# Input tiles at one place modulo 256 bytes, and entries with plain fp32 products, in a two-layer decoder trunk

## The chip, the cores and the metric

The kernel runs on one core of one Trainium2 chip. The metric is the time of one execution on the device in microseconds (us); the smaller the better. Each kernel is run several times and the median is given.

## What is computed

The reference is a causal decoder trunk of two layers on 256 tokens of width 2048, in fp32. Each layer is a mixer and an MLP with a squared relu, each behind an RMS norm with a shift, a scale and a gate from a conditioning vector:

```python
def sqrelu_mlp(h, w1, w2):
    return jnp.square(jax.nn.relu(h @ w1)) @ w2

cond = jax.nn.silu(c)
for l in range(DEPTH):                      # 2
    mod = cond @ ada_w[l] + ada_b[l]        # 2048 -> 6 * 2048
    sh1, sc1, g1, sh2, sc2, g2 = [m[:, None, :] for m in jnp.split(mod, 6, axis=-1)]
    h = rms_norm(x, norm1_g[l]) * (1.0 + sc1) + sh1
    if l % 2 == 0:                          # mLSTM and retention heads
        y = mlstm_retention_mixer(h, even_w_in[e], ..., even_w_out[e])
    else:                                   # sparse attention, 16 query heads
        y = dsa_mixer(h, odd_w_in[o], ..., rel_bias, odd_w_out[o])
    x = x + g1 * y
    h = rms_norm(x, norm2_g[l]) * (1.0 + sc2) + sh2
    x = x + g2 * sqrelu_mlp(h, mlp_w1[l], mlp_w2[l])     # 2048 -> 8192 -> 2048
return x
```

Nearly all of the work is in the linear maps: the input and output projections of the two mixers, the two MLPs, and the conditioning's `ada_w`.

## The kernel before

**Split products.** The kernel computes in a transposed layout: a tile has 128 features on the partitions and the T = 256 tokens in the free dimension. fp32 values are split into a high part in fp32r (a type of four bytes, whose matmuls leave one record each in the trace, where plain fp32 leaves two) and the remainder, also in fp32r. An input tile `hs` (`hs_tile`, L201) holds the high part of 128 features in columns 0 to 255 and the low part in columns 256 to 511. A weight load (`wload`, L235) brings a `raw` tile of 128 x 1024 by DMA on SP's queue; `wsplit` (L226) makes `wh` of it on ScalarE (L230) and `wl` on VectorE (L232). A product is then hi x hi + hi x lo + lo x hi, made by matmuls that all pass through `mm` (L124), in three forms:

- `tmul` (L247), in the MLPs: `wh` stays in the array (the stationary tile), and the 512 columns of `hs`, high and low, stream past it; then `wl` against the 256 high columns. Two matmuls, of 512 and of 256 columns.
- `nmul2` (L281), in the other linear maps and for the last column tiles of the MLP's w2: three matmuls of 256 columns (`wh` x high, `wh` x low, `wl` x high).
- `nmul` (L308), in the last product (`result`, L597: the second MLP's w2, so that the output stands by token) and in the value projections (`linear_n`): a piece of `hs` of 128 columns is stationary, and 512 columns of `wh` or `wl` stream past it. Three matmuls of 512 columns.

`linear` (L252) walks over the contraction index k, one or two k for each weight load, and lets a batch of two loads wait for each other at the end (`stag`).

**Stages.** Layer 0's projections and heads, its output projection (`residual`, `out_groups`), MLP 0 (`mlp`: w1 in 16 groups of 512 columns, then w2 in two groups of eight column tiles), layer 1's projections and attention, its output projection, MLP 1 (w1, then `result`). Between them stand three *entries* (`entry`, L499): the first group of MLP 0's w1, of layer 1's input projection and of MLP 1's w1. At an entry the RMS norm is not known yet, so the first 8 k are multiplied without it: `Norm.plain` makes tiles u = x times a scale column, with the two parts of the shift beside them as two more columns, and `umul` (L494) does three matmuls of 258, 256 and 258 columns. The result is scaled by the norm afterwards, and the shift's sums are added (L532, L533, L537). `Norm.lengths` computes the norm with two tiny matmuls of `ssq` and one of `diag` (L196). The other 8 k come as usual.

**Where tiles lie.** Pools hand out fixed slots in SBUF. `hsp` has 16 slots for `hs` tiles, used in turn; a tile is 2T + 2 floats long (the two columns of the shift), which makes a slot of 2080 bytes, so that the 16 slots start at 224, 0, 32, 64, 96, 128, 160 and 192 modulo 256 bytes, each on two of them, and successive tiles go down by 32. The tags `raw`, `wh` and `wl` have four slots each, all of which start at 224 modulo 256. These places are read from the program as built.

**Order.** Each engine runs its instructions in the order in which the scheduler put them at build time; a tile's slot is written again only when its last reader is done. `Fill` (a generator of conditioning work: DMAs `ada`, and VectorE folds `acc`, L395) is called once for each weight load and spreads a given number of folds over a given number of calls, its `slots`.

Of the kernel before, what the change touches and what calls it, by code (L numbers as in the profile page):

```python
# [18 lines left out]
P = 128  # L19
# [75 lines left out]
def tile_trunk(ctx: ExitStack, tc: tile.TileContext, io, out):  # L95
# [105 lines left out]
    def hs_tile():  # L201
        return hsp.tile([P, 2 * T + 2], F32R, tag="hs", name="hs")

    def split_to_hs(src):
        h = hs_tile()
        S.copy(h[:, 0:T], src)  # L206
        V.tensor_tensor(h[:, T:2 * T], src, h[:, 0:T].bitcast(F32), op=OP.subtract)  # L207
        return h
# [16 lines left out]

    def wsplit(raw, n):  # L226
        wh = wp.tile([P, 1024], F32R, tag="wh", name="wh")
        wl = wp.tile([P, 1024], F32R, tag="wl", name="wl")
        with tc.high_priority(offset=60):
            S.copy(wh[:, :n], raw[:, :n])  # L230
            with held_back():
                last_split[0] = V.tensor_tensor(wl[:, :n], raw[:, :n], wh[:, :n].bitcast(F32), op=OP.subtract)  # L232
        return wh, wl

    def wload(W, k0, kper, cols):  # L235

        w = sum(c1 - c0_ for c0_, c1 in cols)
        raw = wp.tile([P, 1024], F32, tag="raw", bufs=4, name="raw")
# [6 lines left out]
        return wsplit(raw, kper * w)  # L245
# [189 lines left out]
    class Norm:  # L435
# [17 lines left out]
        def plain(self, l, n):  # L453


            sh = shift(l, 3 * n)
            s2 = small.tile([P, 8, 2], F32R, tag="sh2", bufs=1, name="sh2")
            S.copy(s2[:, :, 0], sh[:, 0:8])
            V.tensor_tensor(s2[:, :, 1], sh[:, 0:8], s2[:, :, 0].bitcast(F32), op=OP.subtract)
            us = []  # L460
            for k in range(8):
                u, a = hs_tile(), acol[:, l, n, k:k + 1]
                S.activation(u[:, 0:T], xT[:, k, :], AF.Copy, scale=a)
                S.copy(u[:, T:T + 2], s2[:, k, :].bitcast(F32))
                V.scalar_tensor_tensor(u[:, T + 2:], xT[:, k, :], a, u[:, 0:T].bitcast(F32), op0=OP.mult, op1=OP.subtract)
                us.append(u)
# [27 lines left out]
    def umul(o, u, wh, wl, c, m, start, stop):  # L494
        mm(o[0:m, 0:T + 2], wh[:, c:c + m], u[:, 0:T + 2], start=start, stop=False)
        mm(o[0:m, 0:T], wh[:, c:c + m], u[:, T + 2:2 * T + 2], start=False, stop=False)
        mm(o[0:m, 0:T + 2], wl[:, c:c + m], u[:, 0:T + 2], start=False, stop=stop)

    def entry(W, cols, tiles, norm, l, n, held, late, out, done, fill):  # L499
# [4 lines left out]
        ws = {}  # L504

        def load(k0):
            ws[k0] = wload(W, k0, 2, cols)
            fill()

        for k0 in (0, 2, 4):  # L510
            load(k0)
        norm.lengths(last_split[0].ins)
        hs, sums_ = [None] * KT, []
        for k0 in range(0, KT, 2):
            if k0 not in ws:
                load(k0)
            wh, wl = ws[k0]
            for q, (c, m) in enumerate(tiles):
                for kk in range(2):
                    k = k0 + kk  # L520
                    if k < 8:
                        umul(held[q], us[k], wh, wl, kk * w + c, m, k == 0, k == 7)
# [3 lines left out]
            if k0 == 6:  # L526
                for k in range(8, KT):
                    hs[k] = norm.normed(l, n, k)
                for q, (c, m) in enumerate(tiles):
# [3 lines left out]
                    V.tensor_tensor(s[0:m], b[0:m, T + 1:T + 2], s[0:m], op=OP.add)  # L533
# [91 lines left out]
    def mlp(l, before, fill, norm):  # L625
        with ExitStack() as es:
# [13 lines left out]
            def squared(i, a):  # L640
# [3 lines left out]
            free[:] = [3]  # L644
            hs = entry(io["mlp_w1"][l], [(0, 512)], [(j * P, P) for j in range(4)], before, l, 1,
                       [bank(0), bank(1), bank(2), lbank()], [lbank(), lbank()], [ztile(i) for i in range(4)],
                       lambda q: squared(q, z[q]), fill)
# [11 lines left out]
            if l == 1:  # L659
                fill.flush()  # L660
                while pending:
                    side()
                result(io["mlp_w2"][l], lambda k: split_to_hs(z[k]))
                return
            residual(io["mlp_w2"][l], DFF // P, lambda k: split_to_hs(z[k]), shift(l, 5), norm, mlp_groups(),
                     2, fill)
            fill.flush()
# [25 lines left out]
    with ExitStack() as es:  # L693
# [3 lines left out]
        def wraw(name="raw"):  # L697
            tag = turns.pop(0)
            turns.append(tag)
            return wp.tile([P, 1024], F32, tag=tag, bufs=4, name=name)  # L700
# [477 lines left out]
    mlp(0, before, Fill([(0, 5), (1, 0), (1, 1), (1, 3), (1, 4)], 256), nrm)  # L1178


    fill = Fill([(1, 2)], 60)
    wO = io["odd_w_in"][0]
    with ExitStack() as es:
# [24 lines left out]
        def evac_s(j):  # L1208
# [13 lines left out]
            else:  # L1222
                tb = bank()
                for t in range(2):
# [5 lines left out]
                   lambda q: evac_s(q // 2) if q % 2 else None, fill)  # L1230
# [133 lines left out]
    mlp(1, nrm, Fill([(1, 5)], 70), None)  # L1364
# [32 lines left out]
```

## Time and profile before

| | before |
|---|---|
| median of 3 runs | 2370.38 us (2368.48 to 2370.61) |
| the profiled execution's time | 2370.61 us |
| its span in the trace | 2368.8 us |
| TensorE busy (PE) | 2296.0 us, 97% |
| loads of stationary tiles (PEld, beside PE) | 2038.9 us, 86% |
| VectorE busy (DVE) | 1728.2 us, 73% |
| ScalarE busy (ACT) | 1201.5 us, 51% |
| DMA from memory | 607.38 MB, 257 GB/s over the span |
| mean granted TensorE clock | 0.991 |

Busy times are sums over the instructions of an engine; PE and PEld run side by side. The span goes from the first to the last instruction, and the time of the execution has 1.8 us more around it.

### The profile page before, as it was taken

The numbers are of one execution on the slowest core, as the hardware profiler recorded it, in microseconds if no ns is written. First come the engines' busy times: TensorE is split into PE (matmuls) and PEld (weight loads), VectorE is DVE, ScalarE is ACT, GpSimd is POOL, SyncE is SP. The second block draws the span as 40 slices with busy tenths as digits, with TensorE's granted clock in tenths as the row PEclk, the third lists the DMA queues.
The fourth block names the chain that finished last, engine by engine and source line by source line (L and its number), as shares of the span: only waits on it lengthen the run. The fifth ranks groups of instructions, "written<-read, shape, count | busy, mean of one in ns | idle before, by whom it ended". The sixth has DMA issues, their size and how long they took to land.

```text
span 2368.8 us, 37770 instructions
## 1 busy us (share of the span) xinstructions
PE 2296.0 (97%) x14217; PEld 2038.9 (86%) x14217; DVE 1728.2 (73%) x2550; ACT 1201.5 (51%) x2263; POOL 0.5 (0%) x8
## 2 busy tenths in 40 slices
PE   5899989999999999999999999999999999999999
PEld 3688878999888888899999989999888888888887
DVE  6768897895977777887988889866867456454545
ACT  3235554454556555655555446665655556444442
POOL 0000000000000000000000000000000000000000
PEclk8999999999999999999999999999999999999999
DMA  9998998996698988888898886645887666555554
GB/s 332 361 300 290 305 311 278 328 306 200 214 332 299 309 299 304 300 303 301 284 323 302 255 267 227 213 153 171 276 285 252 181 188 185 191 185 192 188 186 159
DMA packets 268911, 611.99 MB, mean 258 GB/s; under 512 B 26692, under 2 KB 95286, under 8 KB 268728
## 3 DMA queue, kind: packets, MB, share of 16 engines
q1 hardware_dynamic: 268728, 609.59, 77.4%
q8 instruction: 111, 1.82, 0.3%
q14 instruction: 72, 0.59, 0.1%
HBM read 607.38 MB, written 2.12 MB: 257 GB/s over the span
## 4 chain that ended last, share of the span: by engine, by line
PE 79%; DVE 11%; DMA 6%; issue 2%; ACT 2%; SPq 0%; DVEq 0%; ACTq 0%
PE L L124 46%; PE M L124 31%; DVE wl L232 3%; DMA raw<-in_even_w_in_dram 2%; DMA ada<-in_ada_w_dram 2%; DVE acc L395 2%; DVE acc L756 1%; PE M L325 1%; ACT wh L230 1%; DMA raw<-in_mlp_w_dram 1%; DVE hs L490 1%; DVE half L487 1%; DVE cv L1066 0%; DMA xn<-in_x_dram 0%; DMA raw<-in_even_w_out_dram 0%
## 5 line engine op out<-in xcount | busy, mean ns | idle before, releaser
L232 DVE TENSOR_TENSOR wl<-raw,wh 128x1024 fp32r<-128x1024 f32 (+2 forms) x736 | 890.9, 1212 | 521.8 <-ACT wh L230 516.4
L230 ACT CAST wh<-raw 128x1024 fp32r<-128x1024 f32 (+2 forms) x736 | 765.8, 1041 | 881.8 <-PE M L124 460.4
L124 PE MATMUL L<-hs,wh 128*128 128x256 f32 (+2 forms) x4704 | 1154.3, 324 | 7.1 <-ACT wh L230 4.7
L124 PE MATMUL L<-hs,wl 128*128 128x256 f32 (+1 forms) x3168 | 891.2, 282 | 11.2 <-DVE wl L232 11.2
L124 PEld LDWEIGHTS L<-hs,wh 128*128 128x128 f32 x4704 | 781.9, 189 | 76.3 <-ACT wh L230 5.4
L124 PEld LDWEIGHTS L<-hs,wl 128*128 128x128 f32 x3168 | 601.1, 190 | 16.5 <-DVE wl L232 14.4
L124 PE MATMUL M<-hs,wh 128*128 128x256 f32 (+3 forms) x1912 | 544.8, 347 | 0.0
L124 PE MATMUL M<-hs,wl 128*128 128x256 f32 (+2 forms) x1492 | 418.9, 281 | 0.0
L395 DVE SCALAR_TENSOR_TENSOR acc<-ada,cond,acc 128x1024 f32<-128x1024 f32 x300 | 383.4, 1278 | 17.4 <-DMA ada<-in_ada_w_dram 17.0
L124 PEld LDWEIGHTS M<-hs,wh 128*128 128x128 f32 (+1 forms) x1912 | 329.4, 187 | 55.3 <-issue 1.6
L124 PEld LDWEIGHTS M<-hs,wl 128*128 128x128 f32 (+1 forms) x1492 | 279.7, 188 | 2.0 <-issue 0.8
L124 PE MATMUL L<-wh,hs 128*128 128x512 f32 x640 | 213.6, 395 | 0.0
L124 PE MATMUL M<-wh,hs 128*128 128x512 f32 x560 | 188.0, 394 | 0.0
L124 PEld LDWEIGHTS L<-wh,hs 128*128 128x128 f32 x640 | 120.3, 188 | 28.1 <-issue 0.3
L124 PE MATMUL L<-wl,hs 128*128 128x512 f32 x320 | 126.7, 396 | 0.3 <-DVE wl L232 0.3
L124 PEld LDWEIGHTS M<-wh,hs 128*128 128x128 f32 x560 | 105.4, 188 | 24.9
L124 PE MATMUL M<-wl,hs 128*128 128x512 f32 x280 | 110.7, 396 | 0.0
L328 ACT ACTIVATE junk<-M 128x128 f32<-128x128 f32 x210 | 55.0, 276 | 88.9 <-PE M L325 88.9
L756 DVE SCALAR_TENSOR_TENSOR acc<-ar,cond,acc 128x512 f32<-128x512 f32 x120 | 90.2, 751 | 4.8 <-DMA ar<-in_ada_w_dram 1.1
L206 ACT CAST hs<-z 128x256 fp32r<-128x256 f32 x192 | 76.7, 402 | 16.0 <-PE M L124 16.0
L207 DVE TENSOR_TENSOR hs<-z,hs 128x256 fp32r<-128x256 f32 x192 | 78.8, 419 | 1.6 <-ACT hs L206 1.5
L124 PEld LDWEIGHTS L<-wl,hs 128*128 128x128 f32 x320 | 60.2, 188 | 14.4 <-DVE wl L232 1.0
(264 smaller groups left out, 1318.4 us busy)
## 6 DMA issues: line engine op xcount, KB each, us to landing
raw<-in_mlp_w_dram SPq DMA_DIRECT2D x512, 512.0 KB, 4.5
ada<-in_ada_w_dram SPq DMA_DIRECT2D x320, 512.0 KB, 5.3
raw<-in_even_w_in_dram SPq DMA_DIRECT2D x136, 256.0 KB, 5.3
ar<-in_ada_w_dram SPq DMA_DIRECT2D x64, 512.0 KB, 7.7
raw<-in_odd_w_in_dram SPq DMA_DIRECT2D x48, 512.0 KB, 4.8
raw<-in_even_w_out_dram SPq DMA_DIRECT2D x32, 512.0 KB, 4.6
raw<-in_odd_w_out_dram SPq DMA_DIRECT2D x32, 512.0 KB, 4.0
raw<-in_even_w_in_dram SPq DMA_DIRECT2D x28, 512.0 KB, 5.8
```

Of the source, the lines that this page charges most:

```text
L124: PE.matmul(o, a, b, start=start, stop=stop, skip_group_check=True)
L206: S.copy(h[:, 0:T], src)
L207: V.tensor_tensor(h[:, T:2 * T], src, h[:, 0:T].bitcast(F32), op=OP.subtract)
L230: S.copy(wh[:, :n], raw[:, :n])
L232: last_split[0] = V.tensor_tensor(wl[:, :n], raw[:, :n], wh[:, :n].bitcast(F32), op=OP.subtract)
L325: PE.transpose(b[:, i * P:(i + 1) * P], t, ident)
L328: S.activation(j, b[:, i * P:(i + 1) * P], func, accum_out=dst[:, i:i + 1])
L395: V.scalar_tensor_tensor(acc, r, cond[:, kr:kr + 1], acc, op0=OP.mult, op1=OP.add)
L487: V.scalar_tensor_tensor(t, xT[:, k, :], acol[:, l, n, k:k + 1], self.rb, op0=OP.mult, op1=OP.mult)
L490: V.scalar_tensor_tensor(h[:, T:2 * T], t, sh[:, k:k + 1], h[:, 0:T].bitcast(F32), op0=OP.add, op1=OP.subtract)
L756: V.scalar_tensor_tensor(acc, ar[:, kr], cc, acc, op0=OP.mult, op1=OP.add)
```

## The change

All `hs` tiles become 2T floats long, 2048 bytes, so that every slot starts at 224 modulo 256. `wh` slots get 64 more floats, 4352 bytes; in the MLPs the tile is placed 48 floats (192 bytes) into its slot, at 160 modulo 256, and elsewhere at 224. The last product takes its `hs` tiles from the MLP's own pool (`zh`, three slots, also at 224, which the pad of 24 floats brings about), with `wh` at 224 again. The entries' first 8 k become plain fp32 matmuls of 257 columns: one shift column in place of two parts, no low part of u, and weights (`wu`) that a DMA puts directly into `wh` and `wl` slots through `wfetch`, without a split. `entry` no longer calls `fill`, and the three `Fill`s get eight slots less.

```diff
     def hs_tile():
-        return hsp.tile([P, 2 * T + 2], F32R, tag="hs", name="hs")
-
-    def split_to_hs(src):
-        h = hs_tile()
+        return hsp.tile([P, 2 * T], F32R, tag="hs", name="hs")
+
+    def split_to_hs(src, tile=None):
+        h = hs_tile() if tile is None else tile
...
+    place = [0]
+
     def wsplit(raw, n):
-        wh = wp.tile([P, 1024], F32R, tag="wh", name="wh")
+        wh = wp.tile([P, 1024 + 64], F32R, tag="wh", name="wh")[:, place[0]:place[0] + 1024]
         wl = wp.tile([P, 1024], F32R, tag="wl", name="wl")
...
-    def wload(W, k0, kper, cols):
+    def wfetch(raw, W, k0, kper, cols):
...
+        return raw
+
+    def wload(W, k0, kper, cols):
+
+        raw = wp.tile([P, 1024], F32, tag="raw", bufs=4, name="raw")
+        wfetch(raw, W, k0, kper, cols)
+        return wsplit(raw, kper * sum(b - a for a, b in cols))
...
         def plain(self, l, n):
-            sh = shift(l, 3 * n)
-            s2 = small.tile([P, 8, 2], F32R, tag="sh2", bufs=1, name="sh2")
-            S.copy(s2[:, :, 0], sh[:, 0:8])
-            V.tensor_tensor(s2[:, :, 1], sh[:, 0:8], s2[:, :, 0].bitcast(F32), op=OP.subtract)
             us = []
             for k in range(8):
-                u, a = hs_tile(), acol[:, l, n, k:k + 1]
-                S.activation(u[:, 0:T], xT[:, k, :], AF.Copy, scale=a)
-                S.copy(u[:, T:T + 2], s2[:, k, :].bitcast(F32))
-                V.scalar_tensor_tensor(u[:, T + 2:], xT[:, k, :], a, u[:, 0:T].bitcast(F32), op0=OP.mult, op1=OP.subtract)
+                u = hsp.tile([P, 2 * T], F32, tag="hs", name="hs")
+                S.activation(u[:, 0:T], xT[:, k, :], AF.Copy, scale=acol[:, l, n, k:k + 1])
+                S.copy(u[:, T:T + 1], shift(l, 3 * n)[:, k:k + 1])
                 us.append(u)
             return us
...
-    def umul(o, u, wh, wl, c, m, start, stop):
-        mm(o[0:m, 0:T + 2], wh[:, c:c + m], u[:, 0:T + 2], start=start, stop=False)
-        mm(o[0:m, 0:T], wh[:, c:c + m], u[:, T + 2:2 * T + 2], start=False, stop=False)
-        mm(o[0:m, 0:T + 2], wl[:, c:c + m], u[:, 0:T + 2], start=False, stop=stop)
...
-        for k0 in (0, 2, 4):
-            load(k0)
+        ws = []
+        for k0 in range(0, 8, 2):
+            tag, room = (("wh", 1088), ("wl", 1024))[k0 // 2 % 2]
+            r = wp.tile([P, room], F32, tag=tag, bufs=4, name="wu")
+            ws.append(wfetch(r, W, k0, 2, cols))
         norm.lengths(last_split[0].ins)
         hs, sums_ = [None] * KT, []
         for k0 in range(0, KT, 2):
-            if k0 not in ws:
-                load(k0)
-            wh, wl = ws[k0]
+            if k0 >= 8:
+                wh, wl = wload(W, k0, 2, cols)
...
                     if k < 8:
-                        umul(held[q], us[k], wh, wl, kk * w + c, m, k == 0, k == 7)
+                        mm(held[q][0:m, 0:T + 1], ws[k0 // 2][:, kk * w + c:kk * w + c + m], us[k][:, 0:T + 1],
+                           k == 0, k == 7)
...
             free[:] = [3]
+            place[0] = 48
             hs = entry(io["mlp_w1"][l], [(0, 512)], [(j * P, P) for j in range(4)], before, l, 1,
...
-                result(io["mlp_w2"][l], lambda k: split_to_hs(z[k]))
+                place[0] = 0
+                zp.tile([P, 24], F32, name="pad")
+                result(io["mlp_w2"][l],
+                       lambda k: split_to_hs(z[k], zp.tile([P, 2 * T], F32R, tag="zh", bufs=3, name="zh")))
...
-    mlp(0, before, Fill([(0, 5), (1, 0), (1, 1), (1, 3), (1, 4)], 256), nrm)
-    fill = Fill([(1, 2)], 60)
+    mlp(0, before, Fill([(0, 5), (1, 0), (1, 1), (1, 3), (1, 4)], 248), nrm)
+    fill = Fill([(1, 2)], 52)
...
-    mlp(1, nrm, Fill([(1, 5)], 70), None)
+    mlp(1, nrm, Fill([(1, 5)], 62), None)
```

On TensorE, at the place where the first layer's output projection ends and MLP 0's entry begins, the row before is this (M_6080 and M_6081 are banks of PSUM that hold the entry's column tiles; a name is output, then the streamed tile, then the stationary one; x2 means twice in a row):

```order
L124 MATMUL L<-hs,wl 128x256
L124 MATMUL M_6080<-hs,wh 128x258
L124 MATMUL M_6080<-hs,wh 128x256
L124 MATMUL M_6080<-hs,wl 128x258
L124 MATMUL M_6080<-hs,wh 128x258
L124 MATMUL M_6080<-hs,wh 128x256
L124 MATMUL M_6080<-hs,wl 128x258
```

and the same place of the changed kernel is this:

```order
L124 MATMUL L<-hs,wl 128x256
L124 MATMUL M_6080<-hs,wu 128x257 x2
L124 MATMUL M_6081<-hs,wu 128x257 x2
L124 MATMUL M_6082<-hs,wu 128x257 x2
L124 MATMUL L<-hs,wu 128x257
L124 MATMUL M_6122<-c_78,ssq 128x1 x2
L124 MATMUL L<-hs,wu 128x257
L124 MATMUL M_6080<-hs,wu 128x257 x2
L124 MATMUL M_6081<-hs,wu 128x257
L124 MATMUL M_6137<-diag,c_78 128x256
```

Each triple has become one matmul on an unsplit tile; the norm's two `ssq` matmuls stand behind seven of them, and `diag` behind ten.

On SP, which issues the DMAs, the queue ahead of the same entry reads so before (`raw<-in_mlp_w` are loads of MLP weights, `ada` those of the conditioning):

```order
L242 DMA raw<-in_even_w_out_dram 128x1024 x16
L242 DMA raw<-in_mlp_w_dram 128x2x512 x7
L388 DMA ada<-in_ada_w_dram 128x1024
L242 DMA raw<-in_mlp_w_dram 128x2x512 x4
L388 DMA ada<-in_ada_w_dram 128x1024
```

and so in the changed kernel:

```order
L243 DMA raw<-in_even_w_out_dram 128x1024 x16
L243 DMA raw<-in_mlp_w_dram 128x2x512 x4
L243 DMA wu<-in_mlp_w_dram 128x2x512 x4
L243 DMA raw<-in_mlp_w_dram 128x2x512 x8
L395 DMA ada<-in_ada_w_dram 128x1024
```

The entry's four loads for the first 8 k are now `wu`, and they stand behind the four `raw` loads of its other 8 k.

## Rows read from the trace of the kernel before

**Rows 1.** The page: busy time of each engine, the granted clock in 40 slices (tenths), and the chain that ended last by line.
```profile
PE 2296.0 (97%) x14217; PEld 2038.9 (86%) x14217; DVE 1728.2 (73%) x2550; ACT 1201.5 (51%) x2263; POOL 0.5 (0%) x8
...
PEclk8999999999999999999999999999999999999999
...
PE L L124 46%; PE M L124 31%; DVE wl L232 3%; DMA raw<-in_even_w_in_dram 2%; DMA ada<-in_ada_w_dram 2%; DVE acc L395 2%; DVE acc L756 1%; PE M L325 1%; ACT wh L230 1%; DMA raw<-in_mlp_w_dram 1%; DVE hs L490 1%; DVE half L487 1%; DVE cv L1066 0%; DMA xn<-in_x_dram 0%; DMA raw<-in_even_w_out_dram 0%
```

**Rows 2.** The timeline of MLP 0's w1: start in us from the span's start, duration, engine, line, operation, out<-in, shape. Matmuls overlap: a matmul's duration is longer than the time to the next one's start.
```profile
644.26 0.40 PE L124 MATMUL L<-hs,wh 128*128 128x512 f32 x1
644.26 0.19 PEld L124 LDWEIGHTS L<-hs,wl 128*128 128x128 f32 x1
```

**Rows 3.** TensorE by windows in the last product, each one step of 24 matmuls of 512 columns: stretch, length, busy time (records), granted clock, share of the DMA engines' time, GB/s. The steps' `hs` tiles lie at 64, 224, 192 and 160 modulo 256 in the order of the rows, which makes the distance (start of the streamed weights at 224, less start of the `hs` tile that is loaded) 160, 0, 32 and 64. The last row sums over eight steps in a row, one for each place.
```profile
2212.50:2218.11 5.61, 5.61 (x25) 1.00 0.54 186
...
2229.31:2234.78 5.47, 5.47 (x25) 1.00 0.56 180
2234.78:2240.38 5.60, 5.60 (x26) 1.00 0.63 212
2240.38:2245.88 5.50, 5.50 (x25) 1.00 0.53 175
...
sum 44.58, PE 44.58; mean PE 5.57
```

**Rows 4.** The timeline of TensorE inside the step at distance 0 of rows 3; 15 matmuls start from the first of these rows up to the start of the second (x2: two in the row).
```profile
2230.47 0.62 PE L124 MATMUL L<-wh,hs 128*128 128x512 f32 x2
...
2233.87 0.62 PE L124 MATMUL M<-wh,hs 128*128 128x512 f32 x2
```

**Rows 5.** Windows in layer 1's output projection, each one step of 24 matmuls of 256 columns on one `hs` tile: stretch, length, then busy time (records) of PE, PEld, DVE, ACT and POOL, granted clock, DMA share, GB/s. Here `hs` streams and weights at 224 are loaded; the tiles lie at 32 and 224, the distances are 64 and 0. The sum is over eight steps.
```profile
1608.02:1610.85 2.83, 2.83 (x27) 2.83 (x25) 1.62 (x2) 1.54 (x3) 0.00 (x0) 1.00 0.56 179
...
1613.65:1616.53 2.88, 2.88 (x26) 2.88 (x25) 1.62 (x2) 1.54 (x3) 0.00 (x0) 1.00 0.57 182
...
sum 22.77, PE 22.77 PEld 22.77 DVE 11.40 ACT 10.35 POOL 0.00; mean PE 2.85 PEld 2.85 DVE 1.42 ACT 1.29 POOL 0.00
```

**Rows 6.** The timeline of TensorE inside the step at distance 0 of rows 5; 12 matmuls start from the first of these rows up to the second.
```profile
1614.73 0.40 PE L124 MATMUL L<-hs,wh 128*128 128x256 f32 x2
...
1616.17 0.40 PE L124 MATMUL L<-hs,wh 128*128 128x256 f32 x2
```

**Rows 7.** TensorE's waits at the three entries (MLP 0, then three rows for layer 1, then MLP 1): waiting instruction, what it waited for, us in total, times, the longest.
```profile
PE L L124 <- DVE wl L232: 4.1, 2, 3.3
...
PE L L124 <- DVE wl L232: 2.8, 1, 2.8
PE M L124 <- DVE diag L196: 1.1, 1, 1.1
PE L L124 <- ACT shs L532: 0.8, 1, 0.8
...
PE L L124 <- DVE wl L232: 1.8, 1, 1.8
```

**Rows 8.** Windows (columns as in rows 5) of 5 us behind the first and the second entry, where the granted clock is below 1.
```profile
640.00:645.00 5.00, 5.00 (x21) 4.31 (x21) 5.00 (x5) 1.04 (x1) 0.00 (x0) 0.62 0.93 308
1375.00:1380.00 5.00, 5.00 (x34) 5.00 (x34) 5.00 (x5) 1.05 (x1) 0.00 (x0) 0.74 0.94 327
```

**Rows 9.** Windows (columns as in rows 5) of two stretches of layer 0's input projection, 142 and 177 matmuls of 256 columns each.
```profile
326.01:342.71 16.70, 16.70 (x143) 16.70 (x143) 15.82 (x39) 4.21 (x4) 0.00 (x0) 1.00 0.95 330
385.03:405.86 20.83, 20.83 (x180) 20.83 (x178) 19.64 (x38) 6.58 (x11) 0.00 (x0) 1.00 0.92 303
```

**Rows 10.** Windows (columns as in rows 5) in MLP 0's w1, each the matmuls on one weight load, eight pairs of 512 and 256 columns; one of four that follow each other, and their sum.
```profile
809.44:812.26 2.82, 2.82 (x19) 2.47 (x18) 2.82 (x4) 2.79 (x7) 0.00 (x0) 1.00 0.74 209
...
sum 11.20, PE 11.20 PEld 9.79 DVE 8.87 ACT 8.13 POOL 0.00; mean PE 2.80 PEld 2.45 DVE 2.22 ACT 2.03 POOL 0.00
```

**Rows 11.** Windows (columns as in rows 5) in MLP 0's w2, each one step on one `hs` tile, six pairs and two triples; the tiles lie at 0, 224 and 128, the distances are 32, 0 and 160. The sum is over eight steps in a row, one for each place.
```profile
1125.27:1128.05 2.78, 2.78 (x20) 2.54 (x19) 2.73 (x4) 1.36 (x2) 0.00 (x0) 1.00 0.82 231
1128.05:1130.85 2.80, 2.80 (x21) 2.54 (x19) 2.71 (x4) 1.35 (x2) 0.00 (x0) 1.00 0.91 332
...
1136.51:1139.29 2.78, 2.78 (x20) 2.53 (x19) 2.65 (x4) 1.36 (x2) 0.00 (x0) 1.00 0.85 245
sum 22.46, PE 22.46 PEld 20.38 DVE 18.47 ACT 10.84 POOL 0.00; mean PE 2.81 PEld 2.55 DVE 2.31 ACT 1.36 POOL 0.00
```

**Rows 12.** The timeline of TensorE at layer 1's entry; three triples of `umul` start from the first row up to the second.
```profile
1344.40 0.41 PE L124 MATMUL L<-hs,wh 128*128 128x258 f32 x2
...
1345.49 0.40 PE L124 MATMUL L<-hs,wh 128*16 128x258 f32 x2
```

**Rows 13.** A window (columns as in rows 5) at the kernel's start, where the first input projection multiplies plain fp32 tiles of 256 columns; each such matmul leaves two records, so this is eight of them.
```profile
68.10:71.55 3.45, 3.45 (x17) 3.05 (x16) 0.00 (x0) 0.00 (x0) 0.00 (x0) 1.00 1.10 348
```

**Rows 14.** The page: the groups of the two splits and of the folds (line, engine, operation, out<-in, shapes, count, busy us, mean ns, idle before and its releaser), and the loads of MLP weights (count, KB each, median us from issue to landing).
```profile
L232 DVE TENSOR_TENSOR wl<-raw,wh 128x1024 fp32r<-128x1024 f32 (+2 forms) x736 | 890.9, 1212 | 521.8 <-ACT wh L230 516.4
L230 ACT CAST wh<-raw 128x1024 fp32r<-128x1024 f32 (+2 forms) x736 | 765.8, 1041 | 881.8 <-PE M L124 460.4
...
L395 DVE SCALAR_TENSOR_TENSOR acc<-ada,cond,acc 128x1024 f32<-128x1024 f32 x300 | 383.4, 1278 | 17.4 <-DMA ada<-in_ada_w_dram 17.0
...
raw<-in_mlp_w_dram SPq DMA_DIRECT2D x512, 512.0 KB, 4.5
```

More of the change, by code (lines that the diff above doesn't have):

```diff
@@ L233, in wsplit @@
         return wh, wl
-    def wload(W, k0, kper, cols):
+    def wfetch(raw, W, k0, kper, cols):
         w = sum(c1 - c0_ for c0_, c1 in cols)
-        raw = wp.tile([P, 1024], F32, tag="raw", bufs=4, name="raw")
         rv = raw[:, :kper * w].rearrange("p (k c) -> p k c", k=kper)
@@ L244, in wload @@
             o += b - a
-        return wsplit(raw, kper * w)
+        return raw
[3 more added lines that the diff above has]
+        return wsplit(raw, kper * sum(b - a for a, b in cols))
     def tmul(o, h, wh, wl, c, m, start, stop):
@@ L492, in normed, with entry @@
             return h
-    def umul(o, u, wh, wl, c, m, start, stop):
-        mm(o[0:m, 0:T + 2], wh[:, c:c + m], u[:, 0:T + 2], start=start, stop=False)
-        mm(o[0:m, 0:T], wh[:, c:c + m], u[:, T + 2:2 * T + 2], start=False, stop=False)
-        mm(o[0:m, 0:T + 2], wl[:, c:c + m], u[:, 0:T + 2], start=False, stop=stop)
-    def entry(W, cols, tiles, norm, l, n, held, late, out, done, fill):
+    def entry(W, cols, tiles, norm, l, n, held, late, out, done):
         w = sum(b - a for a, b in cols)
         us = norm.plain(l, n)
[L504 to L508, printed above, removed]
-        for k0 in (0, 2, 4):
-            load(k0)
+        ws = []
[3 more added lines that the diff above has]
+            ws.append(wfetch(r, W, k0, 2, cols))
         norm.lengths(last_split[0].ins)
@@ L532, in entry @@
                     S.copy(s[0:m], b[0:m, T:T + 1])
-                    V.tensor_tensor(s[0:m], b[0:m, T + 1:T + 2], s[0:m], op=OP.add)
                     sums_.append(s)
@@ L644, in mlp @@
             free[:] = [3]
+            place[0] = 48
             hs = entry(io["mlp_w1"][l], [(0, 512)], [(j * P, P) for j in range(4)], before, l, 1,
                        [bank(0), bank(1), bank(2), lbank()], [lbank(), lbank()], [ztile(i) for i in range(4)],
-                       lambda q: squared(q, z[q]), fill)
+                       lambda q: squared(q, z[q]))
             if l == 1:
@@ L666, in mlp @@
                      2, fill)
+            place[0] = 0
             fill.flush()
@@ L699, in wraw @@
             turns.append(tag)
-            return wp.tile([P, 1024], F32, tag=tag, bufs=4, name=name)
+            return wp.tile([P, 1088 if tag == "wh" else 1024], F32, tag=tag, bufs=4, name=name)[:, 0:1024]
         xn = [[wraw("xn") for _ in range(2)] for _ in range(2)]
@@ L1229, in tile_trunk @@
                    nrm, 1, 0, [lbank() for _ in range(4)], [bank(0), bank(1)], (kT, vT, ik, iwT),
-                   lambda q: evac_s(q // 2) if q % 2 else None, fill)
+                   lambda q: evac_s(q // 2) if q % 2 else None)
         hget_ = lambda k: hs[k]
```

## Prediction

> **What bounds the kernel now.** I read the page first: TensorE is busy 2296.0 of the 2368.8 us, its granted clock stands at 9 tenths or more after the first slice, and most of the chain that ended last is matmuls of `mm` (L124) [rows 1]. So two things count: what one matmul takes on average, and the few places where TensorE waits.
>
> For the first I read the timeline of one MLP product: the load of the next stationary tile (PEld) starts with the matmul ahead of it and runs beside it [rows 2]. While TensorE streams one tile, it reads another out of SBUF. The change alters exactly one thing about that pair, where the two start modulo 256 bytes. I call **distance** the start of the streamed tile less the start of the tile that is being loaded, modulo 256. Before, hs tiles start at 224, 0, 32, ..., 192 in turn and weights at 224, so the distance goes through all eight values, step by step; after, it is 0, and 64 where an MLP loads a `wh` tile.
>
> That this matters is seen in the windows of the last product, cut at its steps (24 matmuls of 512 columns each, one hs tile a step). The step at distance 0 takes 5.47 us, the one at 64 takes 5.50, the others 5.59 to 5.61 (two of them shown), mean 5.57, all at full clock and with no order in the DMA share beside them [rows 3]. Inside the step at 0 matmuls follow each other evenly: 15 of them in 3.40 us, 226.7 ns each [rows 4]. The out projection's steps (24 matmuls of 256 columns) go the other way: mean 2.85 us, and 2.88 at distance 0 [rows 5], where 12 matmuls take 1.44 us, 120.0 ns each [rows 6]. So distance 0 is good for 512 columns and bad for 256.
>
> For the waits I read them at the three entries: TensorE waits 4.1, 2.8 and 1.8 us for `wl` splits, and 1.1 and 0.8 us for the normaliser's diag and shs [rows 7]. Behind two of them the clock sags: 0.62 of full speed over 5 us and 0.74 over 5 us [rows 8], 1.9 and 1.3 us lost.
>
> **The change part by part.** The sum is made against the profiled run's 2370.61 us, 1.8 us more than its span and 0.2 above the median.
>
> *Last product.* All 64 steps stand at distance 0 (its hs tiles come from the new `zh` pool, as `place[0]` goes back to 0): 24 x 226.7 ns = 5.44 us for 5.57 [rows 3, 4], 64 x 0.13 = **-8.5 us**. If the tile switch at each step's start costs what it costs now, it is 5.47, and -6.4. The program has 264 more such matmuls (value projections), 232.1 ns now (5.57 / 24), 226.7 after: **-1.4**.
>
> *256-column matmuls outside the MLPs*, all at distance 0 now. The program has 4,492: 1,536 in the out projections at 118.6 ns (2.85 us / 24, [rows 5]) and 2,956 others, which in two long stretches of the first layer's input projection took 16.70 us for 142 and 20.83 us for 177 matmuls, 117.7 ns [rows 9] (the other records there are transposes). At 120.0 ns they lose 1,536 x 1.4 ns = 2.2 and 2,956 x 2.3 ns = 6.8: **+9.0 us**. The low end is 0, if distance 0 settles so only where one hs tile stays for 24 matmuls, as in [rows 6]; no row shows alternating tiles at one distance, and I take 120.0, the only row there is at distance 0.
>
> *w1 of both MLPs* (15 groups x 64 pairs x 2 = 1,920 pairs of one 512- and one 256-column matmul). A step of 8 pairs takes 2.80 us on average, 350.0 ns a pair [rows 10]. After, the 512 streams while `wl` is loaded (distance 0) and the 256 while `wh` is loaded (64). The nearest rows: 226.7 ns for a 512 at 0 [rows 4], and for a 256 at 64 the out step that ran at 64, 2.83 us / 24 = 117.9 [rows 5]. A pair is then 344.6 ns, and 1,920 x 5.4 ns = **-10.4 us**. This is the largest term and the least sure: in those rows only one width streams, here two alternate. Bounds: nothing (pairs stay at 350.0), and 339.2 ns (-20.7), if the 256 gains the 5.4 ns that a 512 gained by the last product's rows, too.
>
> *w2 of the first MLP*: its 128 steps of 6 pairs and 2 triples of 256s take 22.46 us for eight, 2.8075 each, with 2.80 at distance 0 and 2.78 at 32 and 160 [rows 11]. The same prices give 6 x 344.6 + 2 x (117.9 + 120.0 + 117.9) = 2,779 ns, so 128 x 28.5 ns = **-3.7 us**. A check on the method: at distance 0 for everything it gives 6 x 346.7 + 6 x 120.0 = 2,800, and the row has 2.80.
>
> *Entries.* Their first 8 k go as plain fp32: one matmul of 257 columns from the fetched weights in place of the triple `umul`. The triple takes 0.363 us (three in 1.09, [rows 12]); a plain one of 256 columns 0.431 (8 of them, 16 records, in 3.45 us, [rows 13]), so 0.433 for 257. They are 32 a stage, 96 in all: 96 x 0.070 = **+6.7 us**. Gone are the four splits that stood ahead of each entry's products (1.04 us of ScalarE and 1.21 of VectorE each, [rows 14]) and with them the three waits for `wl`, 8.7 us, and the smaller of the two clock sags, 1.3: **-10.0**. The waits for diag and shs are kept, and so is 1.9 of clock. Net -3.3. The weights now come by DMA straight into `wh` and `wl` slots. Those come free when the matmuls four and three loads back are done, 3 and 2 out steps (8.5 and 5.7 us) ahead of the entry, and a load lands 4.5 us after issue [rows 5, 14], so the first lands 4 us ahead and the last 1.2 us ahead. On SP four `raw` loads now stand ahead of them, which wait for splits and not for matmuls, and eight behind; these are wanted after the 32 plain matmuls, 32 x 0.433 = 13.9 us later, which covers a load's 4.5.
>
> *At nothing:* `fill` leaves the entries and runs a little denser (160 folds over 246 calls for 254), behind a VectorE that is busy 73% [rows 1]; without that cover a fold of 1.28 us would stand ahead of a split [rows 14]. The third `zh` buffer: the split of step k waits for the products of k-3, as the `wh` split waits for k-2 already. The wider `wh` slot and the pad cost space only.
>
> Sum: -8.5 - 1.4 + 9.0 - 10.4 - 3.7 - 3.3 = -18.3, and 2370.6 - 18.3 = **2352 us**.
>
> A page of the Trainium skill speaks against this: "SBUF — State Buffer", section "SBUF: two separate sides", says that "PE, ACT, and DVE's dedicated pair never wait on anyone". By it no address could move a matmul; the sum would be the entries' -3.3 alone and the time 2367 us, not 2352. The steps of 5.47 and 5.60 us at one clock [rows 3] don't fit it, as far as a TensorE that reads twice counts as one reader.
>
> **The rivals.**
> - *Alignment does nothing*: the 5.47 belongs to something else that comes round with the rotation of the hs tiles, and only the entries remain, 2370.6 - 3.3 = 2367 us. Against it: the order of the steps turns round between 512 and 256 columns at the same distance [rows 3, 5], which a cause outside of TensorE's two reads would hardly do. Chance 0.03.
> - *MLP pairs don't settle*: 512 and 256 columns alternate, each pair restarts the pattern, and pairs stay at 350.0. The 10.4 and 3.7 us are not won: 2366 us. For it: w2's best distances are 32 and 160, not 0 [rows 11], so a mix has an order of its own. Chance 0.12.
> - *The 120 ns is not reached outside the MLPs* with alternating tiles (+9.0 becomes 0: 2343), or the MLP pairs come down to their bound (2352.3 - 10.3 = 2342), or both (2333). For it: the 120.0 was read where one tile stays, and no row shows pairs at a fixed distance. Chance 0.20; I put it at 2342, as one of the two.
> - *Slower: the fetched weights come late.* If the slots are released only when the stage ahead ends, a `wu` load is issued then, lands 4.5 us later, and its three fellows queue on SP behind it; each of the three entries waits 4.5 us and loses 1.9 of clock [rows 8, 14]: 2352.3 + 10.0 (what I took as gone) + 3 x 6.4 = 2382. It decides from a release less than 4.5 us ahead of the first product; I count 8.5 and 5.7. Chance 0.07.
>
> **How the numbers follow.** My forecast has 0.55, with a range of its own of 2344 to 2361 (4 ns either way on 1,920 pairs, with 1 us for the rest). The last 0.03 are mixes of these. About 0.2% (4.7 us, so 2365.6 to 2375.1 around the median) is what a measurement of this kernel can tell from no change. Faster: the forecast, the third rival and the mixes, 0.78. Within 0.2%: the first two rivals, 0.15. Slower: the fourth, 0.07. The range reaches down to 2338, half way between one and both bounds of the third rival, and up to 2367, with the first two; outside are the fourth and the tails.
>
> **What would show it.** The last product's steps should all be 5.44 to 5.47 us, none at 5.60; out steps all 2.88; w1 steps of 8 pairs all of one length, 2.76; w2 steps 2.78. At the entries 8 plain matmuls should take 3.46 us, with no wait for `wl` and none for a DMA of `wu`. TensorE's busy time should fall by about 10 us (the address terms' 15.0 and 1.3 of clock, less 6.7), and its idle time by the 8.7 of the waits. The forecast is wrong if steps of one kind still differ among each other (then it is not the place), if w1 steps stand near 2.80 or well below 2.73, or if the waits list a DMA at the entries.

## The result, and the profile after

The changed kernel takes 2341.13 us, the median of four runs (2338.2 to 2342.12), against 2370.02 us for the kernel before: a ratio of 0.9877, 95% interval 0.9865 to 0.9889, or 29 us less. The forecast was 2352 us, with 2338 to 2367 as its range. The direction was right, and so was that the place of a tile alone moves a matmul; that each matmul has one price by its distance was not. The gain was half as large again as forecast (28.9 for 18.3 us).

The page of the changed kernel, busy times:

```profile
PE 2280.5 (97%) x14121; PEld 2033.0 (87%) x14121; DVE 1704.9 (73%) x2499; ACT 1191.6 (51%) x2248; POOL 0.5 (0%) x8
```

TensorE is still 97% busy. Its busy time fell by 15.5 us [rows 1], the rest of the span by 14.2: two gains of about one size, where 10 and 8.7 were forecast.

To see where they lie, cut both traces at the stages: the first matmul on each weight matrix. Windows of TensorE before (stretch, length, busy time, granted clock, DMA share, GB/s), in the order of the program: layer 0's input and output projections, MLP 0's w1 and w2, layer 1's input and output projections, MLP 1's w1, the last product.

```profile
32.11:497.26 465.15, 437.59 (x2768) 0.97 0.95 314
497.26:596.73 99.47, 96.25 (x801) 1.00 0.70 235
596.73:968.00 371.27, 367.13 (x2152) 0.99 0.86 294
968.00:1332.77 364.77, 364.77 (x2355) 1.00 0.88 300
1332.77:1532.15 199.38, 192.74 (x1567) 0.99 0.74 242
1532.15:1636.44 104.29, 103.96 (x857) 1.00 0.52 162
1636.44:2006.18 369.74, 367.73 (x2160) 1.00 0.70 224
2006.18:2362.92 356.74, 356.74 (x1538) 1.00 0.55 183
```

The same of the changed kernel, with the first stage at the end:

```profile
497.43:595.66 98.23, 96.98 (x801) 1.00 0.73 242
595.66:952.18 356.52, 356.52 (x2121) 1.00 0.88 300
952.18:1312.62 360.44, 359.14 (x2354) 1.00 0.90 309
1312.62:1511.73 199.11, 196.22 (x1530) 1.00 0.73 239
1511.73:1617.49 105.76, 105.49 (x859) 1.00 0.54 165
1617.49:1984.58 367.09, 367.09 (x2129) 1.00 0.70 224
1984.58:2332.95 348.37, 348.37 (x1537) 1.00 0.57 187
32.77:497.43 464.66, 440.84 (x2768) 0.97 0.95 316
```

Half of the gain, 14.8 us, is in MLP 0's w1 with its entry. The same work in MLP 1 gained 2.7. The last product gained 8.4, w2 4.3; the four projections together 0.5 us, and layer 1's input projection holds an entry, too.

Why the two MLPs differ shows inside the stages. Windows of the changed kernel in w1, one weight load of eight pairs each: one in MLP 0, one in MLP 1, then two loads in MLP 1, each with one plain fp32 product of 512 columns (two records) among the pairs (the products that spread the last gate, `ada_rows`), then one more:

```profile
638.47:641.19 2.72, 2.72 (x18) 1.00 1.00 368
...
1729.27:1731.99 2.72, 2.72 (x19) 1.00 0.93 260
1731.99:1735.60 3.61, 3.61 (x21) 1.00 0.94 341
1735.60:1739.25 3.65, 3.65 (x20) 1.00 1.03 379
1739.25:1742.05 2.80, 2.80 (x18) 1.00 0.88 337
```

A step is 2.72 us (340 ns a pair) until the first plain product, apart from steps with transposes in them, and 2.80 (350 ns) from there on; all steps from there to the end of w1, over 80 of them, last 2.80, but for the two in which the other two products stand. Nothing else in the row has changed: the same instructions at the same distances, at full clock. The timeline at the first of these products shows the turn (start, duration):

```profile
1733.35 0.39 PE L124 MATMUL L<-hs,wh 128*128 128x512 f32 x1
1733.58 0.28 PE L124 MATMUL L<-hs,wl 128*128 128x256 f32 x1
1733.69 0.39 PE L124 MATMUL L<-hs,wh 128*128 128x512 f32 x1
...
1734.04 1.02 PE L124 MATMUL M<-acc,c 128*128 128x512 f32 x2
...
1735.24 0.40 PE L124 MATMUL L<-hs,wh 128*128 128x512 f32 x1
1735.48 0.28 PE L124 MATMUL L<-hs,wl 128*128 128x256 f32 x1
1735.60 0.40 PE L124 MATMUL L<-hs,wh 128*128 128x512 f32 x1
```

From 1733.35 to 1733.69 a pair takes 0.34 us, from 1735.24 to 1735.60 0.36 (350 ns, rounded twice).

The other steps came as forecast: one of four steps of the last product, all alike, where [rows 3] has 5.47 to 5.61; and an out step of 2.88, where [rows 5] shows 2.83 and 2.88 in turn.

```profile
2010.63:2016.07 5.44, 5.44 (x25) 1.00 0.58 203
...
1548.38:1551.26 2.88, 2.88 (x27) 1.00 0.63 182
```

At the three entries TensorE's waits of [rows 7] are all gone, those for diag and shs too, and the clock stays at 1.00 (rows two, four and six of the changed kernel's stages above; 0.99 in two of these stages before).

### The profile page after: what moved, and what is told of

The parts are those of the page before. It is cut to its first block, busy times and chain, and to the rows that moved or that the text cites. A ratio compares the mean times of both kernels' runs of the same rounds, so it can differ in the third digit from the quotient of the medians.

```text
span 2339.1 us, 37507 instructions
## 1 busy us (share of the span) xinstructions
PE 2280.5 (97%) x14121; PEld 2033.0 (87%) x14121; DVE 1704.9 (73%) x2499; ACT 1191.6 (51%) x2248; POOL 0.5 (0%) x8
## 4 chain that ended last, share of the span: by engine, by line
PE 80%; DVE 9%; DMA 6%; issue 2%; ACT 2%; SPq 0%; DVEq 0%; ACTq 0%
PE L L124 49%; PE M L124 30%; DMA ada<-in_ada_w_dram 3%; DVE wl L234 3%; DMA raw<-in_even_w_in_dram 2%; DVE acc L402 1%; DVE acc L754 1%; PE M L332 1%; ACT wh L232 1%; DMA raw<-in_mlp_w_dram 1%; ACT junk L335 0%; DVE cv L1064 0%; DVE hs L207 0%; SPq L243 0%; PE M L737 0%
## 5 line engine op out<-in xcount | busy, mean ns | idle before, releaser
L234 DVE TENSOR_TENSOR wl<-raw,wh 128x1024 fp32r<-128x1024 f32 (+1 forms) x724 | 876.7, 1213 | 489.4 <-ACT wh L232 480.1
L232 ACT CAST wh<-raw 128x1024 fp32r<-128x1024 f32 (+1 forms) x724 | 753.7, 1042 | 830.6 <-PE M L124 442.1
L124 PE MATMUL L<-hs,wh 128*128 128x256 f32 (+1 forms) x4608 | 1131.7, 324 | 6.5 <-ACT wh L232 4.2
L124 PE MATMUL L<-hs,wl 128*128 128x256 f32 x3120 | 874.8, 281 | 2.4 <-DVE wl L234 2.4
L124 PE MATMUL M<-hs,wh 128*128 128x512 f32 (+2 forms) x1816 | 518.6, 347 | 0.0
L124 PEld LDWEIGHTS M<-hs,wl 128*128 128x128 f32 (+2 forms) x1444 | 269.2, 186 | 1.9 <-issue 1.0
L124 PE MATMUL L<-wh,zh 128*128 128x512 f32 x512 | 168.7, 389 | 0.0
L124 PE MATMUL M<-wh,zh 128*128 128x512 f32 x512 | 168.6, 389 | 0.0
L124 PE MATMUL L<-wl,zh 128*128 128x512 f32 x256 | 99.7, 389 | 0.0
L124 PE MATMUL M<-wl,zh 128*128 128x512 f32 x256 | 99.6, 389 | 0.0
```

The source lines that it names most:

```text
L124: PE.matmul(o, a, b, start=start, stop=stop, skip_group_check=True)
```

## Experiments

Each is told with the forecast that stood before it ran. The time of the kernel before was 2371.4, 2368.7 and 2371.0 us in the three sittings.

**e1_entries_only: the places undone.**

```diff
-        return hsp.tile([P, 2 * T], F32R, tag="hs", name="hs")
+        return hsp.tile([P, 2 * T + 2], F32R, tag="hs", name="hs")
...
-            place[0] = 48
+            place[0] = 0
...
-                       lambda k: split_to_hs(z[k], zp.tile([P, 2 * T], F32R, tag="zh", bufs=3, name="zh")))
+                result(io["mlp_w2"][l], lambda k: split_to_hs(z[k]))
```

> The changed kernel with its places undone: hs and u tiles are 2T + 2 floats again and rotate through eight places, wh is at 224 everywhere, the last product takes its hs tiles from the common pool. The plain entries stay. If the forecast's price of the entries (-3.3 us) is right: 2367 us. If the entries give 8 to 9 us, as the stages of the two traces suggest: 2361 to 2362 us, with w1 steps of 2.77 to 2.82 us, last-product steps of 5.47 to 5.60 us again and no wait for wl at the entries. If places do nothing: 2341 us, as the changed kernel.

Measured: 2365.9 us, ratio 0.9975 (0.9963 to 0.9988). So the entries are worth 6 us (0.25% of 2370; 2.8 to 8.8 by the interval), and the places the other 23 (0.9975 against 0.9877). The stages of this kernel, third, fourth, seventh and eighth:

```profile
596.04:962.04 366.00, 366.00 (x2120) 1.00 0.86 292
962.04:1327.91 365.87, 365.08 (x2354) 1.00 0.89 304
...
1630.23:1999.76 369.53, 369.53 (x2129) 1.00 0.68 222
1999.76:2356.49 356.73, 356.73 (x1538) 1.00 0.52 183
```

Against these the places gave 9.5, 5.4, 2.4 and 8.4 us; the entry of MLP 0 gave 5.3 of its stage's 14.8.

**e6_last_only: the last product's tiles alone, in the kernel before** (a `zh` pool and a pad of 8 floats, which puts them at 224).

```diff
...
-                result(io["mlp_w2"][l], lambda k: split_to_hs(z[k]))
+                zp.tile([P, 8], F32, name="pad")
+                result(io["mlp_w2"][l],
+                       lambda k: split_to_hs(z[k], zp.tile([P, 2 * T], F32R, tag="zh", bufs=3, name="zh")))
```

> The kernel before with one thing of the change: the last product's hs tiles from a pool of its own at 224, so that all its steps stand at distance 0. All of its 64 steps should take 5.44 us: 8.3 us less, 2362 to 2363 us. If the 5.47 came from the rotation itself and not from the place: steps near 5.57 us and 2370 us.

Measured: 2359.62 us, ratio 0.9963 (0.9948 to 0.9978), 8.8 us less; its last product takes 348.35 us, for 356.74:

```profile
2004.23:2352.58 348.35, 348.35 (x1537) 1.00 0.54 187
```

So the forecast's first term stands by itself, and the address is the cause. The pool of three slots came with it, but the pool is not what does it: in e5 below the same pool stands beside weights that are moved, and no setting that shifts them reaches the 226.7 ns.

**e2_place0: every distance 0.**

```diff
-            place[0] = 48
+            place[0] = 0
```

> The changed kernel with wh at 224 in the MLPs too (the 192 bytes undone), so that every distance is 0. If the price of a matmul goes by its distance alone (226.7 ns for 512 columns and 120.0 for 256 at distance 0): w1 pairs of 346.7 ns, steps of 2.77 us in both MLPs; w2 steps 2.80 us; together 6.1 us lost in the first w1, 0.9 won in the second and 5.1 lost in w2: 2351 us. If the 192 bytes do nothing: 2341 us.

Measured: 2359.73 us, ratio 0.9951 (0.9934 to 0.9967), 9 us worse than expected. The price by distance fails here: a step early in MLP 0's w1 and one later, at the same places:

```profile
624.54:627.36 2.82, 2.82 (x18) 1.00 0.62 190
...
841.84:844.61 2.77, 2.77 (x19) 1.00 0.48 124
```

2.77 us is the 346.7 ns a pair that the distances give; but up to 839 us most steps take 2.82 or 2.83 (353.3 ns a pair), a repeating sequence of 233, 117, 241, 120, 236 and 113 ns between starts. The turn comes at a group of transposes for the conditioning (earlier ones had left the pattern as it was). So there are several patterns at one pair of places here, too, and w2 (370 us for 360) stays in the slow one: nearly all its steps take 2.84 us, where the price by distance says 2.80.

**e3_rows_late: the plain products taken out of w1.**

```diff
         def end():
+            part(0)
             part(1)
             grow[hf] = acc
-            open_.pop(0)
-        open_.append(acc)
-        pending.extend([None] * 2 + [lambda: part(0), None, None, None, end])
+        rows_late.append(end)
+    rows_late = []
...
+                for f in rows_late:
+                    f()
                 place[0] = 0
```

> The changed kernel with the four plain fp32 products of 512 columns that spread the last gate (ada_rows) taken out of MLP 1's w1 and put behind it. Theory A, two patterns at the same places: w1 runs at 340 ns a pair until the first of these products knocks it into 350, where it stays for 87 of 120 steps. Without them all steps take 2.72 us: 87 x 0.08 = 7.0 us less, 2334 us. Theory B, something else in MLP 1 (its VectorE work, its DMA share or its tiles) makes 350: 2341 us, and the steps still turn from 2.72 to 2.80 us in the same place.

Measured: 2335.78 us, ratio 0.9855 (0.984 to 0.987). MLP 1's w1 takes 359.1 us, 8.0 less, all its steps 2.72; the last product, at whose start the four products now stand, 3.3 more. Theory A holds, by the steps; the intervals of the two ratios overlap, 0.984 to 0.987 and 0.9865 to 0.9889. The profiled run adds something: MLP 0, whose instructions are those of the changed kernel, begins in the slow pattern this time and leaves it at the first transposes (steps of this kernel on both sides of them):

```profile
690.18:692.98 2.80, 2.80 (x19) 1.00 0.88 318
...
699.40:702.12 2.72, 2.72 (x19) 1.00 0.87 288
```

So which pattern a stage starts in differs from run to run of the same code.

**e10_turn_after: transposes moved behind the plain products.**

```diff
             grow[hf] = acc
             open_.pop(0)
+            pending.extend([None] * 2 + turn(2 + hf))
...
-                for c in range(4):
+                for c in range(2):
```

> The changed kernel with two of the four `turn`s (eight transposes each) of MLP 1 moved behind the two places where the plain products of ada_rows stand. Theory A, two patterns: the plain products knock w1 from 340 into 350 ns a pair, and a later disturbance can knock it back. If transposes do that: 2.72 us steps again after each turn, 6 to 7 us less, 2334 to 2335 us. If only the plain products matter and nothing brings the row back: 2341 us, steps of 2.80 us from the first of them to the end.

Measured: 2338.02 us, ratio 0.9864 (0.9848 to 0.9881). In w1 it does what theory A says: a step ahead, two with the plain products, one with transposes, and one behind:

```profile
1734.99:1737.71 2.72, 2.72 (x18) 1.00 0.79 261
1737.71:1741.32 3.61, 3.61 (x20) 1.00 0.75 252
1741.32:1744.98 3.66, 3.66 (x20) 1.00 0.47 139
1744.98:1748.58 3.60, 3.60 (x26) 1.00 0.93 325
1751.40:1754.12 2.72, 2.72 (x18) 1.00 0.98 355
```

The transposes bring the row back, both times, and w1 takes 360.3 us for 367.1. By the medians that is 3 us and not 6 to 7; the interval reaches from 2333 to 2341 us, so the time alone would not tell it from no gain. The profiled run, the slowest of the four, won these 6.7 us in w1 and lost 5.8 in layer 0's input projection, whose instructions are those of the changed kernel (470.46 us, in the row here, for 464.66):

```profile
31.82:502.28 470.46, 444.06 (x2769) 0.96 0.94 312
```

**e4_wide48: the 192 bytes outside the MLPs, too** (`place = [48]`, and 0 around the value projections).

> The changed kernel with wh 192 bytes on outside the MLPs too, for the 256-column products (distance 64 where wh is loaded, 0 where wl is), and at 224 for the value projections and the last product. If the price goes by the distances, as in the entries' triples of the MLPs of the changed kernel (116.3 ns a matmul there, 119.8 outside): 4,100 x 3.5 ns = 14 us at most, part of it hidden in layer 0 by waits that grow, so 2327 to 2336 us, out-projection steps of 2.79 us. If a triple of 256s does not care: 2341 us and steps of 2.88 us.

Measured: 2338.3 us, ratio 0.9861 (0.9847 to 0.9876). That is outside the 2327 to 2336 that were expected. The two matmuls of a triple that multiply by `wh` came down to about 116.5 ns between starts, but the one by `wl` stayed at 120.2; I had priced all three by the cheaper kind. Nor is that the split which the distances give: beside the matmul by `wl` the next `wh` is loaded, the distance 64 that was to be cheap, and beside the second one by `wh` the `wl`, at distance 0. The mean is 117.7, so 8 us of matmul time, of which the stages show 3.6.

**e5_map: places that change during the run** (`wh` and `wl` each 0 to 224 bytes past the place of `hs`; one run). It is e3_rows_late with `wl` slots 64 floats longer and one `rows` buffer less.

```diff
+        i = {"w1a": n0 // 3, "w1b": 40 + n0 // 3, "w2": n0 // 2, "o0": n0, "o1": 32 + n0, "last": n0 // 2}.get(stage)
+        PA, PB = (place[0], 0) if i is None else (8 * (i % 8), 8 * (i // 8 % 8))
```

> A map and not a version: the kernel of e3_rows_late, in which the places of wh and of wl (0 to 224 bytes past their slots' start, in steps of 32) change during the run: every third load in w1 of both MLPs, every second in w2, every load in the out projections, every step in the last product; each pair of places comes up once or more. If the price goes by the distance of each matmul alone, steps sort into rows and columns: 512 columns beside a load of wl are shortest at wl place 0 (226.7 ns), 256 beside a load of wh cheapest at wh place 192, and their prices add. If a row of matmuls settles as a whole into one of several patterns, steps at the same pair of places differ in the two MLPs by up to 14 ns a pair (340 against 347 to 354), and a pair of places other than (192, 0) reaches 340 ns too. In the out projections I expect 2.80 to 2.88 us a step, the least near wh and wl both at 224 (distance 32).

Measured: 2361.48 us in its one run. In w1 the settled pairs take 343.8 to 355 ns in all settings, mostly 346.7, 350 or 353.3, and never 340; at (192, 0), `wh` first, they took 350 in both MLPs, while w2's at the same places took 340 in this very run. In the last product no setting with a shift came below 228.8 ns a matmul, where the changed kernel has 226.7. The surprise is in the out projections. Two steps of 24 matmuls, at (64, 64) and then (96, 64):

```profile
553.40:556.12 2.72, 2.72 (x26) 1.00 0.77 264
556.12:558.98 2.86, 2.86 (x27) 1.00 0.77 246
```

At (64, 64), and again at (64, 192), matmuls of 256 columns follow each other every 113.3 ns. I had expected the least near 32. Before, steps at the distance that this is (192, `hs` less weights) took 2.83 us.

**e11_all_places: a version from the map.** As e3_rows_late, with `wl` slots 64 floats longer and one `rows` buffer less as well.

```diff
-    place = [0]
+    place = [16, 16]
...
-        wl = wp.tile([P, 1024], F32R, tag="wl", name="wl")
+        wl = wp.tile([P, 1024 + 64], F32R, tag="wl", name="wl")[:, place[1]:place[1] + 1024]
...
+            place[:] = [48, 0]
             for g in range(1, DFF // 512):
...
```

> What the map suggests as a version: rows late as in e3_rows_late; in the triples of 256 columns outside the MLPs wh and wl both lie 64 bytes past the place of hs (where the map's out steps fell into 113.3 ns a matmul, 2.72 us, in both places where it tried that wh place with wl 64 or 192), in the MLPs wh 192 bytes and wl 0, in the value projections and the last product all at one place. If that pattern takes hold with alternating hs tiles too: 4,492 x 6.5 ns = 29 us of TensorE's time less than e3_rows_late, of which layer 0's input projection may give back about half of its 12 us to waits: 2308 to 2318 us, out steps 2.72 us. If the pattern needs one hs tile for many matmuls: the out projections alone, 1,536 x 6.6 ns = 10 us: 2325 us. If it is not reached at all (2.83 us an out step): 2332 us.

Measured: 2328.29 us, ratio 0.9814 (0.9798 to 0.983), faster than both kernels, but 10 us short of the best case. The pattern takes hold with alternating tiles, too: in layer 1's two projections the 256s come down to 114 ns, and its output projection from 105.8 to 103.2 us. But it has a slower twin: two steps of layer 0's output projection ahead of a disturbance (a wait of 2.2 us, behind it transposes and a granted clock of 0.72 over 6 us), one behind it.

```profile
514.17:516.89 2.72, 2.72 (x26) 1.00 0.80 227
516.89:519.61 2.72, 2.72 (x26) 1.00 1.00 380
541.50:544.33 2.83, 2.83 (x27) 1.00 0.56 187
```

It stays at 2.83 to the end of that stage, which takes 100.73 us; in e12, with the same instructions and nearly the same wait there, but with the clock at 1.00, the steps return to 2.72 and the stage takes 96.56. Part of the 4.2 us between them is the clock. And layer 0's input projection does not follow at all: its 1,852 matmuls of 256 columns went from 119.7 to 114.8 ns, 9 us, and the stage from 464.66 to the first row below. The second row is the same stage of e12, with the same places there as e11, the third that of e3, with those of the changed kernel:

```profile
32.99:497.31 464.32, 431.99 (x2768) 0.98 0.95 315
...
32.86:499.83 466.97, 434.48 (x2768) 0.97 0.95 314
...
32.04:497.97 465.93, 439.98 (x2769) 0.98 0.95 314
```

TensorE's busy time fell by 8.9 us there and its waits took that up. One of them is for ScalarE's normalised heads; before, after and in e11:

```profile
PE M L1014 <- ACT yn L1006: 7.8, 4, 3.7
```

```profile
PE M L1012 <- ACT yn L1004: 3.6, 4, 1.9
```

```profile
PE M L1016 <- ACT yn L1008: 8.8, 4, 2.7
```

A single wait is loose evidence: with the places of the kernel before this one is 5.0 us in e1 and 5.7 in e6, with those of the changed kernel 4.9 to 5.9 in e2, e3, e5 and e10. The length of the stage says more. Over the profiled runs it is 462.7 to 465.2 us where the tiles rotate (the kernel before, e1, e6), 462.8 to 470.5 where all stand at distance 0 (the changed kernel, e2, e3, e5, e10) and 464.3 and 467.0 in e11 and e12: it does not follow the spacing of the matmuls. What sets it was not tested; the DMA engines' share is 0.94 or 0.95 there in every run.

**e12_triples: e11 with w1 as three matmuls of 256 columns**, `wh` and `wl` both 64 bytes past the place of `hs`.

```diff
-                            f = tmul if len(tl) == 1 else nmul2(q)
+                            f = wmul if tri else tmul if len(tl) == 1 else nmul2(q)
```

> e11_all_places with w1 of both MLPs multiplied as three matmuls of 256 columns at those places (wh and wl 64 bytes on) in place of one of 512 and one of 256. If the pattern of 113.3 ns holds there, a triple takes 340 ns, as a pair in its better pattern: the time of e11_all_places within 3 us. If triples with h tiles that alternate stay near 118 ns: 354 ns each, 1,920 x 14 ns = 27 us more.

Measured: 2332.1 us, ratio 0.983 (0.9811 to 0.9848). w1 takes 359.4 and 357.5 us, for 356.2 and 357.1 of e11. MLP 0 begins in the slow pattern, some 28 steps of 2.83 us, and leaves it at the first transposes; from there on a triple in the good pattern costs what a pair costs in its own (eight in a step):

```profile
616.93:619.76 2.83, 2.83 (x27) 1.00 0.69 184
699.71:702.43 2.72, 2.72 (x27) 1.00 0.84 278
```

## Why the forecast was right, and where it was off

The time lies in the stated range, but not in the forecast's own, 2344 to 2361 us: 2341 is where the third rival stood (2342). And two of the three signs that I had named for being wrong came up in w1. Its steps still differ among each other, 2.72 and 2.80 us at the same distances, where one length of 2.76 was forecast; and 2.80 is what MLP 1 has for most of them. By the prediction's own words that would mean that it is not the place. e1 and e6 show that it is; the sign was wrong, because it took for granted that a place has one price. By the terms, the misses hardly cancel, but for the two MLPs inside the w1 term, and add up to the 11 us:

- *Last product, -8.5*: -8.4 by the stages, -8.8 alone (e6). Right, step by step.
- *The 264 other 512s, -1.4*: 228 to 229 ns between starts for 232.6, so -1.1 of matmul time.
- *w1, -10.4*: -9.5 and -2.4, together -11.9. The sum is near, the working is not: a pair of 344.6 ns does not exist in this kernel. It takes 340 or 350, and the forecast's price stood between by chance: MLP 0 won 4.3 us more than its half of the term, MLP 1 2.8 less. The step that failed is the one that gives a matmul a price by its distance, read from a row in which only one width streams: at one pair of places a pair settles at 340 or 350, at distance 0 at 346.7 or 353.3 (e2), and the distance does not say at which. The bound of 339.2 that I kept was all but reached in MLP 0, and the other bound, 350.0, in most of MLP 1.
- *w2, -3.7*: -5.4 against e1; its pairs mostly stand at 340, its triples near 118 ns a matmul.
- *256s outside the MLPs, +9.0*: the matmuls came out as priced, 119.4 to 120.0 ns between starts, about +8.2 us by their counts. But the four projections lost only 2.6 against e1, with the other 512s in it. This is the largest miss, 5 us, in my step that put every slower matmul on the path that sets the end: the length of layer 0's input projection does not follow the matmuls, as e11 and e12 show from the other side. How much of the 5 us is this and how much the spread of that stage, 462.8 to 470.5 us at the same places, is not shown. I had weighed TensorE's share of the whole span and not that stage's own waits; its busy time is 437.59 of 465.15 us there.
- *Entries, -3.3*: 6 us less by the ratio of e1, whose interval holds the 3.3 as well. The trace tells more: I kept the waits for diag and shs and one of the two clock sags, and all of them went. Over the entry's 53 us the clock before was 0.94 (columns as in rows 5), so the first sag alone was 3.2 us, and I had read 1.9 from one window of 5 us.

```profile
596.73:650.00 53.27, 49.13 (x323) 44.74 (x322) 49.21 (x86) 29.22 (x54) 0.00 (x0) 0.94 0.65 210
```

- The rivals: alignment that does nothing and pairs that stay at 350 are ruled out by e1 and by MLP 0. The late `wu` loads did not come: no entry waits. The third rival, 2342 us, is what happened in the time, through both of its halves in part: MLP 0's pairs almost at their bound, and of the 256s' 8.2 us of matmul time only some 3.7 in the stages.
- The rule weighed in the forecast, of "SBUF — State Buffer" in the Trainium skill, does not carry over to a TensorE that reads two tiles: moving addresses alone is worth 23 us (e1), and 8.8 in the last product by itself (e6). That it is these two reads which hold each other up is the likely reading, and not shown. Another page of the Trainium skill, "TensorE: Matmul & The Clock Gate", section "Step-by-step: what each phase is for", says that loading the next tile does not take read bandwidth from the running matmul; the steps of 5.47 and 5.60 us at one clock [rows 3] differ, and e6 moved the loaded tile alone and took the running 512s from about 232 to 226.7 ns between starts. The measurement decides.

What stays open: what makes the patterns. The runs show that places decide which ones exist and that disturbances choose among them; what TensorE's two reads do to each other inside one was not seen.

## What to carry to other kernels

When matmuls follow each other without a gap, look at the spacing of their starts over a whole stage, not at a mean: a spacing that is constant, and another constant somewhere else at the same places, means patterns, and a term of a sum taken from one of them is a choice between two values and not a price. Try the places of the streamed and of the loaded tile modulo 256 bytes in one run that changes them as it goes; one run found 113.3 ns here where the best guess was 116.7. And before a gain or a loss per matmul is multiplied by a count, check the stage for waits that will take it up.

## What the hardware showed beyond that

- 256 columns beside a load of the next tile take 113.3, about 117.8 or 120.0 ns, 512 take 226.7 or about 232; a pair 340, 346.7, 350 or 353.3, all at full clock. The lowest of each are 1, 2 and 3 times 113.3.
- A row of matmuls stays in its pattern for hundreds of microseconds (MLP 1's last 100 steps in e3, 272 us). One plain fp32 product of 512 columns turned 340 into 350 where it first stood in such a row (the changed kernel and e4) and twice in e10, where transposes behind the products turned it back both times; at distance 0 (e2) the same products left 346.7 as it was. The same code starts in either pattern.
- By this, part of the spread between runs of one kernel (2338.2 to 2342.1 us here) can be a choice of pattern: MLP 0's first 26 steps in the slow one cost e3's profiled run 2.1 us.
